# Dividing after the value products, and gathering 40 modulation dot products into the experts' loop

## The chip, the cores and the metric

The kernel runs on one core of a Trainium2 chip. The metric is the device time of one execution in microseconds (us). The engines are called as the profile calls them: PE is TensorE (PEld its weight loads), DVE is VectorE, ACT is ScalarE, POOL is GpSimd, SP is SyncE; "POOL queue" and "SP queue" are the DMA queues that POOL and SP issue to.

## The reference

Two transformer blocks of fp32 over 512 tokens of 1024 features; cut to what matters here:

```python
# first block: attention of 16 heads, 512 + 256 keys, values of 64 features
s = (einsum('bqhd,bkhd->bhqk', qn, kn) + einsum('bqhd,bkd->bhqk', qr, kr)) * ATTN_SCALE
o = einsum('bhqk,bkhd->bqhd', softmax(s), v)
y = (g_a * (o @ w_o_mla) + g_c * conformer_conv(u)) @ w_out
x = x + g1 * y
# experts: 8 heads, each with the 16 best of 128 x 128 single-neuron experts
act = gelu(einsum('thkd,td->thk', u_tab[expert], h2))
x = x + g2 * einsum('thk,thkd->td', gate * act, v_tab[expert])
x = rms_norm(x, final_g)
# second block: two layers, each a mixer and an MLP, all modulated by
mod = silu(c_2) @ ada_w + ada_b            # 2 layers x 6 x 1024
# layer 0's mixer: attention over each query's 128 best keys by an index score
# layer 1's mixer: difference of two softmaxes, by a factor from b_lambda
```

## The kernel before

Nearly all products are of fp32 operands that are split into a rounded part and the rest (`split`: ACT makes the rounded part `hi`, DVE the rest `lo`), and three matmuls make one product (`mm3`, lines 88 to 90). Weights come in chunks of 1 MB [128, 2048] through the SP queue into a ring of 2 raw tiles; three pairs of hi and lo tiles hold the split ones. The program is written as one Python pass with steps that are put in between by hand; a scheduler at build time then fixes each engine's order. The stages in order, with their place in the span: norm and latents (0 to 100 us), convolution and gate projections (to 265), first attention (267 to 500), merge (`merge` 500 to 594, `out_first` 594 to 646), choice of experts (to 790), gates and the first 80 expert tiles' activations made ahead (790 to 1190), the experts' loop (1190 to 1945), and the second block from there.

*First attention* (`attention`, line 656). Eight pairs of heads, each of 4 blocks of 128 queries times 2 heads: 64 steps. `logits` (line 709) makes a block's scores in PSUM; DVE takes the maximum (line 715), ACT the exponential with its sum (717), DVE the sum's reciprocal (718), and then ACT (line 720, for half of the steps) or DVE (line 722) scales the block. Two steps later `trans` (line 725) transposes it on PE (732), ACT copies it out (733) and, once both heads of a block are there, 12 matmuls of 128 columns bring the products with the values (742). After four blocks ACT copies the pair's result out (745). `lam_init` (line 1697), the factor of the second block's difference mixer, follows behind all heads, with the load of its row.

*Division by sums.* The second block's first attention (`dsa_attend`, line 1577) doesn't scale its probabilities: `over_sums` (line 774) divides the result of a pair. DVE makes 8 reciprocals per query, ACT spreads them over 512 columns (778), PE transposes them (782), ACT copies them out (783), and DVE multiplies (784).

*Modulation of the second block.* Layer 0's 6144 modulations are 48 dot products of the 128 partitions: one DVE instruction multiplies a [128, 1024] block of `ada_T` with the row silu(c_2), and adds up. The first 40 of them are made before layer 0 in two places: 22 in `merge` and `out_first` (`row_dots`, line 641; `dots`, line 217; the load is POOL's, 512 KB each, line 225, the product line 230; `DOT_AT` says how many at which step), and 18 in `dsa_attend` (`ws_dots`, line 145, product at line 151), whose blocks come as 9 chunks through the weights' ring. The row of silu(c_2) is made at the merge's start with a table load on ACT (line 214), and goes to scratch `sil2_d` for later use.

*The experts' loop* (`experts`, line 1196). The tokens 128 to 511 go through all 128 tiles of 128 experts: `up` multiplies the tile's activations [128, 384] with the gates (line 1239) and splits them into `ch` and `cl`; `down` makes 18 matmuls of 512 columns with the second table's chunk. The first 48 tiles of the loop also make their activations; the last 80 read theirs back (`sr`, 192 KB each on the SP queue, four tiles ahead). The first 128 tokens go another way, pick by pick (`gather_init`, line 1136): step n loads 128 rows by index on the POOL queue (line 1152) into a ring of 5 tiles, and DVE takes its dot product (1160) or adds it up (1170), four steps (`GLAG`) later. `near` (line 1253) runs `GATHER` steps beside each tile, 2.3 in the first 48 and 0.65 in the last 80; 96 steps are made ahead of the loop, and 256 are all.

## Time and profile before

| | |
|---|---|
| three timed runs | 3270.59, 3274.64, 3274.76 us, median 3274.64 |
| profiled execution | span 3265.6 us; what lies around the span isn't given |
| PE busy | 3150.1 us, 96% |
| DVE busy | 2437.2 us, 75% |
| ACT busy | 1369.8 us, 42% |
| POOL busy | 557.0 us, 17% |
| DMA | 600.71 MB, mean 184 GB/s |

A busy share is an average over stages with different limits, so it says little on one of them. A group of instructions shows its busy time, the mean duration of one, and the idle time of the engine just before them with what ended it. PE's matmuls are pipelined: the duration of one is longer than the time between two starts. A chain is followed back from the last instruction to what released it; its shares are of the stretch that it covers. "Issue" is time in which the engine waited for nothing that the profile shows.

### The profile page before, as it was taken

The numbers are of one execution on the slowest core, as the hardware profiler recorded it, in microseconds if no ns is written. First come the engines' busy times: TensorE is split into PE (matmuls) and PEld (weight loads), VectorE is DVE, ScalarE is ACT, GpSimd is POOL, SyncE is SP. The second block draws the span as 40 slices with busy tenths as digits, with TensorE's granted clock in tenths as the row PEclk, the third lists the DMA queues.
The fourth block names the chain that finished last, engine by engine and source line by source line (L and its number), as shares of the span: only waits on it lengthen the run. The fifth ranks groups of instructions, "written<-read, shape, count | busy, mean of one in ns | idle before, by whom it ended". The sixth has DMA issues, their size and how long they took to land.

```text
span 3265.6 us, 44404 instructions
## 1 busy us (share of the span) xinstructions
PE 3150.1 (96%) x17065; PEld 2701.9 (83%) x17065; DVE 2437.2 (75%) x4498; ACT 1369.8 (42%) x2093; POOL 557.0 (17%) x474
## 2 busy tenths in 40 slices
PE   6999999999999999999999999999999999899998
PEld 5787887889899999999878777769888887798887
DVE  5898899699999987777756676977566757773446
ACT  4225774333356553333333344474322245543221
POOL 1210002002232544333323310000111000000000
PEclk8999999999999999999999999999999999999999
DMA  8551016435789998888978762322566321222221
GB/s 296 187 181 46 1 40 210 176 113 188 250 306 339 321 346 305 292 294 297 328 269 300 275 220 85 110 91 91 188 214 208 132 91 63 74 96 92 78 103 65
DMA packets 181864, 600.71 MB, mean 184 GB/s; under 512 B 17009, under 2 KB 89490, under 8 KB 144659
## 3 DMA queue, kind: packets, MB, share of 16 engines
q1 hardware_dynamic: 127666, 401.76, 34.9%
q0 software_dynamic: 53984, 196.11, 16.9%
q8 instruction: 134, 2.20, 0.3%
q14 instruction: 80, 0.65, 0.1%
HBM read 550.53 MB, written 47.27 MB: 183 GB/s over the span
## 4 chain that ended last, share of the span: by engine, by line
PE 57%; DVE 17%; issue 12%; DMA 6%; ACT 3%; POOL 3%; POOLq 0%; DVEq 0%; ACTq 0%; SPq 0%
PE psp L90 10%; PE psp L88 10%; PE psp L89 10%; PE psd L89 5%; PE psd L90 5%; PE psd L88 5%; DVE lo L101 4%; DMA sr<-s_d 3%; DVE ohc L1128 3%; DVE r L1160 2%; POOL r L1152 2%; DMA r<-in_v_experts_dram,gidx 2%; PE pso L742 2%; DVE ohr L1123 2%; PE psl L88 1%
## 5 line engine op out<-in xcount | busy, mean ns | idle before, releaser
L96 ACT ACTIVATE hi<-raw 128x2048 fp32r<-128x2048 f32 (+2 forms) x263 | 500.9, 1909 | 878.3 <-PE psd L90 282.8
L101 DVE TENSOR_TENSOR lo<-raw,hi 128x2048 fp32r<-128x2048 f32 (+2 forms) x263 | 599.3, 2281 | 226.0 <-ACT hi L96 225.4
L88 PE MATMUL psp<-hT2h,hi 128*128 128x512 f32 (+1 forms) x960 | 360.6, 376 | 4.3 <-ACT r L1556 3.2
L90 PE MATMUL psp<-hT2h,lo 128*128 128x512 f32 (+1 forms) x960 | 359.8, 375 | 1.0 <-DVE lo L101 1.0
L88 PE MATMUL psu<-hT2h,hi 128*128 128x384 f32 x1024 | 356.8, 348 | 3.8 <-ACT r L962 3.8
L89 PE MATMUL psp<-hT2l,hi 128*128 128x512 f32 (+1 forms) x960 | 359.7, 375 | 0.0
L90 PE MATMUL psu<-hT2h,lo 128*128 128x384 f32 x1024 | 348.2, 340 | 0.0
L89 PE MATMUL psu<-hT2l,hi 128*128 128x384 f32 x1024 | 348.0, 340 | 0.0
L89 PE MATMUL psd<-lo,ch 128*128 128x512 f32 x768 | 306.6, 399 | 10.8 <-DVE lo L101 10.8
L90 PE MATMUL psd<-hi,cl 128*128 128x512 f32 x768 | 305.8, 398 | 0.0
L88 PE MATMUL psd<-hi,ch 128*128 128x512 f32 x768 | 305.5, 398 | 0.0
L1152 POOL DMA_INDIRECT r<-in_v_experts_dram,gidx x128 | 198.8, 1553 | 405.0 <-DVE sr L1239 189.4
L1152 POOL DMA_INDIRECT r<-in_u_experts_dram,gidx x128 | 204.0, 1594 | 353.1 <-DVE ohc L1128 130.4
L88 PEld LDWEIGHTS psp<-hT2h,hi 128*128 128x128 f32 x960 | 182.0, 190 | 39.5 <-ACT r L1556 3.6
L90 PEld LDWEIGHTS psp<-hT2h,lo 128*128 128x128 f32 x960 | 181.8, 189 | 35.9 <-DVE lo L101 1.4
L89 PEld LDWEIGHTS psp<-hT2l,hi 128*128 128x128 f32 x960 | 181.9, 189 | 34.0
L89 PE MATMUL psd<-lo,sqh 128*128 128x512 f32 x512 | 202.7, 396 | 0.0
L90 PE MATMUL psd<-hi,sql 128*128 128x512 f32 x512 | 202.7, 396 | 0.0
L88 PE MATMUL psd<-hi,sqh 128*128 128x512 f32 x512 | 202.5, 396 | 0.0
L88 PEld LDWEIGHTS psu<-hT2h,hi 128*128 128x128 f32 x1024 | 194.8, 190 | 5.8 <-ACT r L962 4.7
L89 PEld LDWEIGHTS psu<-hT2l,hi 128*128 128x128 f32 x1024 | 194.8, 190 | 1.0
L90 PEld LDWEIGHTS psu<-hT2h,lo 128*128 128x128 f32 x1024 | 194.1, 190 | 0.0
(565 smaller groups left out, 6847.0 us busy)
## 6 DMA issues: line engine op xcount, KB each, us to landing
raw<-in_u_T_dram SPq DMA_DIRECT2D x64, 1024.0 KB, 6.3
raw<-in_v_p_dram SPq DMA_DIRECT2D x64, 1024.0 KB, 5.7
raw<-in_mlp_dram SPq DMA_DIRECT2D x64, 1024.0 KB, 4.8
dotw<-in_ada_T_dram POOLq DMA_DIRECT2D x78, 512.0 KB, 4.3
gate_d<-gst SPq DMA_DIRECT2D x12, 2048.0 KB, 10.3
gt<-gate_d SPq DMA_DIRECT2D x32, 768.0 KB, 9.6
raw<-in_w_cg_dram SPq DMA_DIRECT2D x16, 1024.0 KB, 5.4
dotw<-in_w_mod_T_dram POOLq DMA_DIRECT2D x32, 512.0 KB, 4.9
```

The source lines that it names most:

```text
L88: mm(out, ah, bh, start=start, stop=False)
L89: mm(out, ah, bl, start=False, stop=False)
L90: mm(out, al, bh, start=False, stop=stop)
L96: ins = nc.scalar.activation(hi, src, AF.Copy)
L101: return nc.vector.tensor_tensor(lo, src, bf(hi), op=OP.subtract)
L742: nc.tensor.matmul(po[64 * r:64 * r + 64, qb * P:(qb + 1) * P], vg[:, kt, c:c + 64], L["PT", r][:, kt], start=kt == 0, stop=kt == 5)
L1123: V.tensor_tensor(rows, iota.unsqueeze(1).to_broadcast([P, 4, P]), pick[0][:, t0:t0 + 4].unsqueeze(2).to_broadcast([P, 4, P]), op=OP.is_equal)
L1128: V.tensor_scalar(col, iota, pick[1][:, t:t + 1], pick[2][:, t:t + 1], op0=OP.is_equal, op1=OP.mult)
L1152: ins = nc.gpsimd.indirect_dma_start(out=got[n], out_offset=None, in_=tab, in_offset=bass.IndirectOffsetOnAxis(ap=self.gidx[:, k:k + 1], a ...
L1160: ins = V.scalar_tensor_tensor(r, r, 1.0, h2, op0=OP.mult, op1=OP.mult, accum_out=act[:, k:k + 1])
```

## The change

1. The first attention leaves its probabilities as the exponential has them. Its sums stay in a tile `sum` per pair, the reciprocals and scalings of lines 718 to 722 are gone, the transposed probabilities of two blocks of queries stand side by side, so that the products with the values have 256 columns, and `over_sums` takes the place of the copy at line 745. The row of lambda is loaded at the attention's start; the scheduler now puts lambda's few instructions into the first norm, the exponential's two table loads with them.
2. `EARLY` is 0 and `MIDDLE` 40: none of the first 40 dot products is left in `merge`, `out_first` and `dsa_attend`. They are steps 256 to 295 of the gather, each a plain load of 512 KB on the POOL queue into the same ring of 5 tiles. The last 80 tiles have 1.17 steps each. The row silu(c_2) is made at the start of `experts` (a load, a sigmoid on ACT with a table load before and after it, a multiplication), and the bias of the first 16 columns is added behind the gather.
3. POOL's DMA scratch is 8192 bytes instead of the default 16384.

```diff
-FILL_P, GATHER, DOT_AT, TAPS = (16, 16, 12, 16), (2.3, 0.65), ((10,), 1, 1, 1, 2), 2
-EACT = (0, 2)
+FILL_P, GATHER, TAPS = (16, 16, 12, 16), (2.3, 1.17), 2
-EARLY = 22
-MIDDLE = range(EARLY, 40, 2)
+EARLY = 0
+MIDDLE = 40
...
     def attention(self, es_o, es_cw):
+        self.lam = self.cp.tile([P, 260], F32, name="lam")
+        self.rows_bcast(self.lam[:, :256], A["b_lambda"])
...
-                st = ep.tile([P, 3], F32, tag="st", name="st", bufs=5)
-                self.pace = nc.vector.reduce_max(st[:, 0:1], pl[:, :, :384], axis=AX.XY, negate=True)
+                st = ep.tile([P, 1], F32, tag="st", name="st", bufs=5)
+                self.pace = nc.vector.reduce_max(st, pl[:, :, :384], axis=AX.XY, negate=True)
+                if i % 8 == 0:
+                    L["sum", p] = ep.tile([P, NT, 2], F32, tag="sum", name="sum")
                 e = ep.tile([P, 2, 384], F32, tag="e", name="e", bufs=EB)
-                nc.scalar.activation(e, pl[:, :, :384], AF.Exp, bias=st[:, 0:1], accum_out=st[:, 1:2])
-                nc.vector.reciprocal(st[:, 2:3], st[:, 1:2])
-                if i % 4 in EACT:
-                    nc.scalar.activation(e, e, AF.Copy, scale=st[:, 2:3])
-                else:
-                    nc.vector.tensor_scalar(e, e, st[:, 2:3], None, op0=OP.mult)
+                nc.scalar.activation(e, pl[:, :, :384], AF.Exp, bias=st, accum_out=L["sum", p][:, qb, r:r + 1])
...
-                PT = L["PT", r] = ep.tile([P, 6, P], F32, tag="PT", name="PT", bufs=3)
+                if qb % 2 == 0:
+                    L["PT", r] = ep.tile([P, 6, 2, P], F32, tag="PT", name="PT", bufs=3)
...
-                if r == 0:
+                if i % 4 < 3:
                     return
                 po, vg = L["po"], vs[p // 2]
+                qs = slice(256 * (qb // 2), 256 * (qb // 2) + 256)
                 for kt in range(6):
                     for r in range(2):
                         c = (2 * p + r) % 4 * 64
-                        nc.tensor.matmul(po[64 * r:64 * r + 64, qb * P:(qb + 1) * P], vg[:, kt, c:c + 64],
-                                         L["PT", r][:, kt], start=kt == 0, stop=kt == 5)
+                        nc.tensor.matmul(po[64 * r:64 * r + 64, qs], vg[:, kt, c:c + 64],
+                                         L["PT", r][:, kt].rearrange("p a n -> p (a n)"), start=kt == 0, stop=kt == 5)
                 if i % 8 == 7:
-                    nc.scalar.activation(o[:, p], po, AF.Copy)
+                    self.over_sums(L.pop(("sum", p)), po, o[:, p], pst)
...
     def gather_init(self, es, h2):
+        middle = self.ada_blocks(EARLY, MIDDLE)
+        total = 2 * P + len(middle)
...
+            got[n] = self.grows.next()
+            if n >= 2 * P:
+                self.after(nc.gpsimd.dma_start(got[n], middle[n - 2 * P]), mybir.DependencyClass.Sync)
+                return
...
+            if n >= 2 * P:
+                j = EARLY + k
+                ins = V.scalar_tensor_tensor(r, r, 1.0, self.sil2, op0=OP.mult, op1=OP.mult,
+                                             accum_out=self.adac[:, 0, j:j + 1])
+                self.after(ins, mybir.DependencyClass.NoSync)
+                return
...
     def experts(self, act):
+            self.sil2 = self.row(ap, A["c_2"], tag="sil2")
             y = ap.tile([P, D], F32, name="py")
+            nc.scalar.activation(y, self.sil2, AF.Sigmoid)
+            V.tensor_tensor(self.sil2, self.sil2, y, op=OP.mult)
+            self.sil2_d = self.dram.tile([1, D], F32, name="sil2_d")
+            nc.sync.dma_start(self.sil2_d, self.sil2[0:1])
...
-                if i % 5 == 2 and i // 5 < len(MIDDLE):
-                    self.ws_dots(row, MIDDLE[i // 5])
...
-    nc = bacc.Bacc("TRN2", target_bir_lowering=False, num_devices=1)
+    nc = bacc.Bacc("TRN2", target_bir_lowering=False, num_devices=1, dynamic_dma_scratch_size=8192)
```

ACT's order within a pair of heads of the first attention, before (`psl` are scores, `e` the probabilities, `PT` the transposed ones, `pso` the products with the values, `o_T` the result):

```order
L717 ACTIVATE e,st<-psl,st 128x768
L720 ACTIVATE e<-e,st 128x768
L733 ACTIVATE PT<-pt 128x384 x2
L717 ACTIVATE e,st<-psl,st 128x768
L733 ACTIVATE PT<-pt 128x384
L717 ACTIVATE e,st<-psl,st 128x768
L720 ACTIVATE e<-e,st 128x768
L733 ACTIVATE PT<-pt 128x384
L745 ACTIVATE o_T<-pso 128x512
L733 ACTIVATE PT<-pt 128x384
```

And now, around the end of a pair (the line numbers are the changed kernel's):

```order
L698 ACTIVATE e,sum<-psl,st 128x768
L712 ACTIVATE PT<-pt 128x3x128 x2
L698 ACTIVATE e,sum<-psl,st 128x768
L712 ACTIVATE PT<-pt 128x3x128 x2
L758 ACTIVATE o_T<-sum 128x512
L712 ACTIVATE PT<-pt 128x3x128 x2
L698 ACTIVATE e,sum<-psl,st 128x768
L763 ACTIVATE o_T<-ptr 128x512
L712 ACTIVATE PT<-pt 128x3x128 x2
L698 ACTIVATE e,sum<-psl,st 128x768
```

The scaling between exponential and copy (line 720) is gone, the copy of the result (745) too, and two instructions of the division by sums stand in their place, the spreading of the reciprocals (758) and the copy of their transposes (763).

DVE's order ahead of the first head pair of `dsa_attend`, before (`raw` are chunks of the stream, `kz0l` and `kz1l` the rest parts of the first pair's keys, `dmask` and `ixm` the choice of the best keys):

```order
L151 SCALAR_TENSOR_TENSOR raw_76,adac<-raw_76,silr_17129 128x1024
...
L151 SCALAR_TENSOR_TENSOR raw_76,adac<-raw_76,silr_17129 128x1024
...
L151 SCALAR_TENSOR_TENSOR raw_75,adac<-raw_75,silr_17129 128x1024
...
L151 SCALAR_TENSOR_TENSOR raw_75,adac<-raw_75,silr_17129 128x1024
...
L1575 MATCH_REPLACE dmask<-ixm_16764,dmask 128x512
L151 SCALAR_TENSOR_TENSOR raw_76,adac<-raw_76,silr_17129 128x1024
L1564 TENSOR_SCALAR dmask<-dmask 128x512
L101 TENSOR_TENSOR kz0l<-psk,kz0h 64x512
L151 SCALAR_TENSOR_TENSOR raw_76,adac<-raw_76,silr_17129 128x1024
L101 TENSOR_TENSOR kz1l<-psk,kz1h 64x512
```

And now:

```order
L100 TENSOR_TENSOR lo_82<-raw_76,hi_79 128x2048
...
L1567 MATCH_REPLACE dmask<-ixm_16489,dmask 128x512
L1566 MAX ixm_16489<-dmask 128x8
L1567 MATCH_REPLACE dmask<-ixm_16489,dmask 128x512
L1556 TENSOR_SCALAR dmask<-dmask 128x512
L100 TENSOR_TENSOR lo_81<-raw_76,hi_78 128x2048
L100 TENSOR_TENSOR kz0l<-psk,kz0h 64x512
L1560 ISA e,st<-psl,bias 128x128
L1560 ISA st 128x1
L100 TENSOR_TENSOR kz1l<-psk,kz1h 64x512
```

The dot products (line 151) are gone from in front of the keys' rest parts; the splits of two chunks of the mixer's output weights (`lo`) have moved up to the same place.

DVE's order in the last 80 tiles of the experts' loop, before (`sr` are activations read back, `gt` gates, `cl` the activations' rest part, `lo` that of a chunk, `gacc` the sum of gathered rows):

```order
L101 TENSOR_TENSOR lo_80<-raw_76,hi_77 128x2048
L101 TENSOR_TENSOR cl_11355<-sr_11362,ch_11350 128x384
L1239 TENSOR_TENSOR sr_11361<-sr_11361,gt 128x384
L1170 SCALAR_TENSOR_TENSOR gacc<-r_8090,gact,gacc 128x1024
L101 TENSOR_TENSOR cl_11356<-sr_11363,ch_11351 128x384
L101 TENSOR_TENSOR lo_81<-raw_75,hi_78 128x2048
L1239 TENSOR_TENSOR sr_11362<-sr_11362,gt 128x384
L101 TENSOR_TENSOR cl_11357<-sr_11364,ch_11352 128x384
L1239 TENSOR_TENSOR sr_11363<-sr_11363,gt 128x384
L1170 SCALAR_TENSOR_TENSOR gacc<-r_8091,gact,gacc 128x1024
L101 TENSOR_TENSOR cl_11353<-sr_11365,ch_11348 128x384
L1239 TENSOR_TENSOR sr_11364<-sr_11364,gt 128x384
```

And now, in the part in which the dot products stand (`sil` is the row silu(c_2)):

```order
L1141 SCALAR_TENSOR_TENSOR r_7727,adac<-r_7727,sil_10979 128x1024
L1141 SCALAR_TENSOR_TENSOR r_7728,adac<-r_7728,sil_10979 128x1024
L1141 SCALAR_TENSOR_TENSOR r_7729,adac<-r_7729,sil_10979 128x1024
L100 TENSOR_TENSOR cl_10998<-sr_11005,ch_10993 128x384
L100 TENSOR_TENSOR lo_80<-raw_76,hi_77 128x2048
L1230 TENSOR_TENSOR sr_11010<-sr_11010,gt 128x384
L100 TENSOR_TENSOR cl_10999<-sr_11006,ch_10994 128x384
L1230 TENSOR_TENSOR sr_11005<-sr_11005,gt 128x384
L1141 SCALAR_TENSOR_TENSOR r_7730,adac<-r_7730,sil_10979 128x1024
L1141 SCALAR_TENSOR_TENSOR r_7731,adac<-r_7731,sil_10979 128x1024
L100 TENSOR_TENSOR cl_11000<-sr_11007,ch_10995 128x384
L1230 TENSOR_TENSOR sr_11006<-sr_11006,gt 128x384
```

Two or three dot products (line 1141) stand where one or two additions of gathered rows (line 1170) did.

## Rows read from the trace of the kernel before

**Rows 1.** Page: the span, busy time of each engine, one of its costliest groups.
```profile
span 3265.6 us, 44404 instructions
...
PE 3150.1 (96%) x17065; PEld 2701.9 (83%) x17065; DVE 2437.2 (75%) x4498; ACT 1369.8 (42%) x2093; POOL 557.0 (17%) x474
...
L101 DVE TENSOR_TENSOR lo<-raw,hi 128x2048 fp32r<-128x2048 f32 (+2 forms) x263 | 599.3, 2281 | 226.0 <-ACT hi L96 225.4
```

**Rows 2.** Busy time by stage: stretch, length; engines' busy us (count); clock, DMA share, GB/s.
```profile
281.00:499.40 218.40, 214.59 (x1687) 176.95 (x1685) 195.33 (x326) 168.87 (x335) 6.54 (x6) 1.00 0.06 23
500.00:594.00 94.00, 92.89 (x418) 76.39 (x419) 85.62 (x122) 31.64 (x30) 22.57 (x25) 1.00 0.62 215
594.00:646.00 52.00, 49.61 (x411) 48.97 (x411) 32.24 (x60) 20.65 (x41) 4.39 (x12) 1.00 0.44 152
1100.00:1200.00 100.00, 100.00 (x654) 99.13 (x653) 91.00 (x199) 57.48 (x56) 49.50 (x22) 1.00 0.92 333
1190.00:1590.00 400.00, 400.00 (x2009) 363.45 (x2008) 285.89 (x294) 137.80 (x149) 143.20 (x105) 1.00 0.85 303
1590.00:1945.00 355.00, 344.15 (x1456) 275.61 (x1455) 240.35 (x260) 114.79 (x124) 105.67 (x56) 0.99 0.83 286
```

**Rows 3.** Waits, 281 to 500 us: who waited for whom, us, times, longest.
```profile
PEld pso L742 <- issue: 9.3, 47, 0.4
PEld pso L742 <- ACT PT L733: 6.9, 25, 0.6
...
DVE lam L1703 <- DMA lam<-in_b_lambda_dram: 1.6, 1, 1.6
```

**Rows 4.** Timeline of TensorE, 433 to 435.2 us: start, duration, engine, line.
```profile
432.72 0.28 PE L89 MATMUL psv<-lo,ckvh 128*128 128x256 f32 x1
...
433.19 0.28 PE L90 MATMUL psv<-hi,ckvl 128*128 128x256 f32 x1
433.40 1.52 PE L742 MATMUL pso<-PT,vg 128*64 128x128 f32 x22
434.86 0.44 PE L88 MATMUL psl<-kcat10h,qT 128*128 128x384 f32 x1
```

**Rows 5.** Groups of 2085 to 2204 us: busy us, mean ns, idle before.
```profile
L1668 PEld LDWEIGHTS pt<-ident,e 128*128 128x128 f32 x160 | 18.9, 140 | 8.0 <-issue 2.9 <-ACT do L783 2.3 <-ACT e L1570 0.8
...
L782 PE MATMUL ptr<-ident,do 128*128 128x128 f32 x32 | 5.2, 281 | 0.7 <-ACT do L778 0.7
...
L778 ACT ACTIVATE do<-sum 128x512 f32<-128x512 f32 x8 | 5.0, 620 | 0.0
...
L784 DVE TENSOR_TENSOR do<-do,pso 128x512 f32<-128x512 f32 x7 | 4.8, 683 | 1.6 <-ACT e L1570 1.2 <-ACT do L783 0.4
```

**Rows 6.** Chain of 267 to 501 us by line, shares of 234 us.
```profile
by line: PE pso L742 22.3%; PE pt L732 14.7%; PE psl L88 10.5%; PE psl L90 9.1%; PE psl L89 8.6%; PE psq L88 3.6%; PE psq L90 2.9%; PE psq L89 2.7%; ACT e L717 2.1%; ACT PT L733 2.1%; ACT e L720 1.8%; PE psv L88 1.6%; DMA lam<-in_b_lambda_d
```

**Rows 7.** Timeline of ScalarE, about 55 us; in brackets the idle time before.
```profile
54.58 0.52 ACT L519 ACTIVATE conv_y<-psq 128x416 f32<-128x416 f32 x1 [1.24 <-PE psq L90]
```

**Rows 8.** Groups of 500 to 646 us (the merge).
```profile
L230 DVE SCALAR_TENSOR_TENSOR dotw<-dotw,silr 128x1024 f32<-128x1024 f32 x22 | 27.8, 1263 | 0.0
...
L214 ACT ACT_TABLE_LOAD x1 | 1.3, 1283 | 0.0
```

**Rows 9.** Chain of 2085 to 2205 us by line, shares of 120 us.
```profile
by line: PE pso L1677 20.8%; PE pt L1668 13.8%; PE psl L88 9.3%; PE psl L89 8.6%; PE psl L90 8.2%; ACT e L1570 6.8%; DVE raw L151 4.7%; PE ptr L782 3.0%; issue 3.0%; DVE lo L101 2.8%; PE psk L88 2.3%; PE psk L89 2.3%; PE psk L90 2.1%; DVE e
```

**Rows 10.** Waits of TensorE, 2085 to 2165 us.
```profile
PE psl L89 <- DVE kz0l L101: 4.1, 1, 4.1
```

**Rows 11.** Waits, 1590 to 1945 us (last 80 expert tiles).
```profile
DVE sr L1239 <- DMA sr<-s_d: 106.7, 42, 6.6
...
PE psd L89 <- DVE lo L101: 10.8, 6, 3.3
```

**Rows 12.** DMA, 1590 to 1945 us: GB/s in 40 slices, and the sum.
```profile
GB/s 311 400 372 340 345 242 212 302 290 239 344 261 282 234 336 266 356 246 280 290 282 283 382 235 246 249 314 269 365 258 205 270 320 225 274 293 236 305 261 213
DMA packets 54280, 101.45 MB, mean 286 GB/s; under 512 B 2992, under 2 KB 42032, under 8 KB 49328
```

More of the change, by code (lines that the diff above doesn't have):

```diff
@@ L142, in ws_split @@
             self.ws_nsplit += 1
-        self.ws_prefetch()
-    def ws_dots(self, row, j0):
-        self.ws_prefetch()
-        t = self.ws_r.pop(self.ws_i)
-        for j in range(2):
-            b = t[:, j * D:(j + 1) * D]
-            self.nc.vector.scalar_tensor_tensor(b, b, 1.0, row, op0=OP.mult, op1=OP.mult,
-                                                accum_out=self.adac[:, 0, j0 + j:j0 + j + 1])
-        self.ws_i += 1
-        self.ws_nsplit += 1
         self.ws_prefetch()
@@ L312, in build @@
             self.mods_rest()
-            dots = self.row_dots("c_2", self.ada_blocks(0, EARLY), self.adac[:, 0], es_y, "left", 2)
-            self.run(dots, DOT_AT[4])
-            self.merge(aT, dots)
+            self.merge(aT)
             xp = self.pool("x")
@@ L318, in build @@
             es_p, es_n = self.peer_open()
-            self.out_first(aT, dots)
+            self.out_first(aT)
             self.bias_rows()
@@ L344, in chunk_list @@
             L += [A[name][i] for i in range(A[name].shape[0])]
-            if name == "a_uv":
-                self.ws_plain += range(len(L), len(L) + len(MIDDLE))
-                L += [A["ada_T"][j // 2] for j in MIDDLE]
         return L
@@ L648, in first @@
             self.silu_row(name, row, dp)
-            if name == "c_2":
-                self.sil2_d = self.dram.tile([1, D], F32, name="sil2_d")
-                self.nc.sync.dma_start(self.sil2_d, row[0:1])
             steps[0]()
@@ L784, in over_sums, with merge @@
         nc.vector.tensor_tensor(dst, dst, po, op=OP.mult)
-    def merge(self, aT, dots):
+    def merge(self, aT):
         nc, A = self.nc, self.A
@@ L839, in evac_a @@
                 ln(j)
-                self.run(dots, DOT_AT[1])
             def evac_c(j, pt):
@@ L846, in evac_c @@
                 self.split(aT[0][:, j], aT[1][:, j], t, hi_eng="dve")
-                self.run(dots, DOT_AT[2])
             self.proj_T(4, aT, psp, evac_a)
@@ L870, in mods_rest, with out_first @@
                               self.pool("modr", es=es))
-    def out_first(self, aT, dots):
+    def out_first(self, aT):
         nc, A, x = self.nc, self.A, self.x
@@ L891, in evac @@
                 self.pace = nc.vector.tensor_tensor(x[t][:, cs], x[t][:, cs], y, op=OP.add)
-                if c == 2:
-                    self.run(dots, DOT_AT[3])
             def block(t):
@@ L909, in out_first @@
             self.proj_tm((1, 3), aT, psp, evac, block)
-            self.run(dots, len(dots))
             self.pace = None
@@ L1144, in gather_init @@
         V = nc.vector
+        middle = self.ada_blocks(EARLY, MIDDLE)
+        total = 2 * P + len(middle)
         got = {}
         def rows(n):
+            got[n] = self.grows.next()
+            if n >= 2 * P:
+                self.after(nc.gpsimd.dma_start(got[n], middle[n - 2 * P]), mybir.DependencyClass.Sync)
+                return
             tab, k = (A["u_experts"], n) if n < P else (A["v_experts"], n - P)
-            got[n] = self.grows.next()
             ins = nc.gpsimd.indirect_dma_start(
@@ L1173, in step @@
         def step(n):
-            if n < 2 * P:
+            if n < total:
                 rows(n)
@@ L1179, in gather_init @@
         self.pace = None
-        self.gsteps = [lambda n=n: step(n) for n in range(2 * P + GLAG)]
+        self.gsteps = [lambda n=n: step(n) for n in range(total + GLAG)]
     def after(self, ins, kind):
@@ L1272, in experts @@
             self.es_g.close()
+            V.tensor_tensor(self.adac[:, 0, :16], self.adac[:, 0, :16], self.adab[:, 0, :16], op=OP.add)
             self.bias_open()
@@ L1588, in dsa_attend @@
             v = kp.tile([P, NT, D], F32, name="dv")
-            row = kp.tile([P, D], F32, name="silr3")
-            self.rows_bcast(row, self.sil2_d)
             for r in range(2):
@@ L1699, in lam_init @@
         nc, V = self.nc, self.nc.vector
-        lam = self.lam = self.cp.tile([P, 260], F32, name="lam")
-        self.after(self.rows_bcast(lam[:, :256], self.A["b_lambda"]), mybir.DependencyClass.Sync)
+        lam = self.lam
         for i in range(2):
```

6 lines of the change are left out of this document (2 added, 4 removed).

## The prediction

> **What bounds the kernel now.** I read the page first. TensorE is busy for 96% of the span and VectorE for 75% [rows 1], so by the average only TensorE seems to matter; what the change can be worth is seen only in the six places that it touches. I read those by the table of stages [rows 2]. Its first line is the first attention: TensorE 214.59 of 218.40 us, VectorE 195.33, ScalarE 168.87. All three are near their limit, so what ends there are short waits of TensorE. The two merge lines (500 to 594 and 594 to 646) leave TensorE 1.11 and 2.39 us idle. Of the experts' loop the first 400 us leave TensorE nothing (400.00 of 400.00, DMA at 303 GB/s), while the last 355 us, in which the activations made ahead are read back, have TensorE at 344.15, VectorE at 240.35, and the DMA engines at a share of 0.83 and 286 GB/s. Then I read each place by its own view: the waits, TensorE's timeline and the chain in the attention [rows 3, 4, 6], the groups of the second block's first attention, which already divides late [rows 5], ScalarE at the start [rows 7], the dot products of the merge [rows 8], chain and waits of the second block's first attention [rows 9, 10], waits and transfers of the experts' last stretch [rows 11, 12].
>
> The profiled execution's span is 3265.6 us [rows 1]; its own time is not given apart. The median of the three runs, 3274.64, lies 9.0 above the span, and I take those 9.0 as what lies around it. A measurement of this kernel can tell about 0.2%, 6.5 us, from no change.
>
> **First attention, products with the values.** 768 products of 128 columns become 384 of 256. TensorE's timeline shows both widths side by side [rows 4]: 22 of the narrow ones start at 433.40 and the next product at 434.86, 66 ns each; the 256-column ones start every 0.1175 us (432.72 to 433.19 in four steps). 768 x 0.066 = 51.0 us become 384 x 0.1175 = 45.1: -5.9. Their weight loads besides sit idle for 9.3 us on issue and 6.9 us on the copies of the transposed probabilities [rows 3]; half the loads, half of it: -8.1, which partly is the same time. I take -7; the ends are -5.9 and -16.2 (all of it).
>
> **Its division.** 64 reciprocals and 64 scalings go, half of these on ScalarE. ScalarE's scalings (line 720) are 1.8% of the chain of 234 us [rows 6], 4.2 us. When they go the next wait there is the copies of line 733, with 2.1% in the same row, so I take half, -2.1; ends -4.2 and 0. VectorE's scalings aren't among the chain's lines shown: nothing, because reduction and exponential of the next block cover them. In return each pair of heads gets the division by sums. The second block's attention has it in the same form [rows 5]: 32 transposes, 5.2 us busy, 0.7 us of waits before them and 2.3 us of waits of the next transposes on its second copy. I take 5.2 and half of the waits, +6.7, because the first attention has the next pair's queries and keys to put in between; ends +5.2 and +8.2. For the last pair nothing covers it: the broadcast, 0.620, and the multiplication, 0.683 [rows 5], +1.3. The attention without the row of lambda: -7 - 2.1 + 6.7 + 1.3 = -1.1.
>
> **The row of lambda** is loaded at the attention's start, no longer behind its last heads, where VectorE waits 1.6 us for it [rows 3]: -1.6. Its exponential now lies in the first norm, between uses of another table, so that ScalarE loads two tables there. One load takes 1283 ns [rows 8], and ScalarE has a gap of 1.24 us at that place [rows 7]: 2.6 - 1.2 = +1.4; ends 0 and +2.6.
>
> **Merge.** 22 dot products, 27.8 us of VectorE [rows 8], and a table load leave these stages. TensorE is idle for only 3.5 us in both together [rows 2], so this is all they can give; I take -2, since some idle time ends on the normalisation itself; ends -3.5 and 0. What is saved on VectorE beyond that was covered by products.
>
> **Second block's first attention.** 18 dots and 9 transfers of 1 MB on SP's queue leave it. The dots are 4.7% of a chain of 120 us [rows 9], 5.6 us. TensorE's one long wait there, 4.1 us, is for the rest part of the first keys (kz0l) [rows 10], ahead of which VectorE's order has five dots. But in the changed order splits of chunks of the output weights have moved up to the same place, one of 2.28 us [rows 1] directly ahead of it. -5.6 + 2.3 = -3.3; ends -5.6 and 0.
>
> **Start of the experts' loop.** A row load on SP's queue, a sigmoid, one multiplication and two table loads (2.6 us, [rows 8]) are new. What queues behind them on ScalarE are the roundings of chunks and of gelu's results; with TensorE at 400.00 of 400.00 [rows 2] the chunks are split ahead of their use, and I take 0; ends 0 and +2.6. Moving the bias of 16 columns costs one small addition behind the loop: 0. The smaller scratch of POOL's DMAs: 0, because no more than five of them are in flight in the loop, by the ring of rows, which stays.
>
> **Last 80 tiles.** All 40 dots come here: 40 x 1.263 [rows 8] = 50.5 us of VectorE, and 40 x 0.524 = 21.0 MB on POOL's queue. VectorE has 115 us free, and waits 106.7 us for activations read back [rows 11], so its time has room. But the transfers rise from 101.45 MB [rows 12] to 122.4. Three ways to price that. (1) The first five slices of this very stretch mean 353.6 GB/s, one of them 400 [rows 12]; at that pace 346 us are enough, less than the 355 of today: 0. (2) TensorE's stalls on split weights, 10.8 us [rows 11], grow with the traffic (1.21) and with VectorE's load (1.21): 15.8, so +5. (3) The pace of the gates' stage, 333 GB/s at a share of 0.92 [rows 2], holds as a ceiling: 368 us, +13. I take the middle one, +5, because the pace of (3) was reached with TensorE at 100.00, which may have been what set it. Ends 0 and, if only the 303 GB/s of the loop's first part are had, +49. In the order two or three dots now stand between a tile's rest part and the next multiplication, where one or two steps of the gather were; each waits for its own row, and a late row holds up the splits behind it.
>
> The Trainium skill, page "DMA: Bandwidth & Descriptors", section "Where 436 GB/s comes from", puts the limit of HBM to SBUF transfers at about 358 GB/s per core. By that figure 122.4 MB are 342 us (an estimate), the term would be 0 and not +5, and the sum 5 us lower. The slice of 400 GB/s [rows 12] already lies above this limit, so the trace doesn't bear it out as a ceiling.
>
> **Sum:** attention -1.1, lambda -1.6 + 1.4, merge -2, second attention -3.3, experts' start 0, last tiles +5: -1.6. The span becomes 3264, the time 3273.0: no change that can be measured.
>
> **The rivals.**
> - *Slower: transfers bound the last 80 tiles.* For it: 0.83 of the DMA engines are taken now, and 1.21 times that is 1.00, where the busiest stages of the trace show 0.92 [rows 2, 12]; 42 of the waits are already for activations read back [rows 11], behind 1 MB chunks on SP's queue. Against it: slices at 340 to 400 GB/s [rows 12]. It decides once the sustained pace falls below 345 GB/s (122.4 MB in 355 us). At 333 the term is +13 and the sum -6.6 + 13 = +6.4, 3281; at 316, halfway to the first part's 303 [rows 2], 387 us, +32 and +25, 3300. Chance 0.30 that the sum passes +6.5.
> - *Faster: the loads fit into the gaps.* DMA at 353 GB/s and VectorE in its 115 us take everything, so the last tiles cost 0, and the attention gives more of the weight loads' waits (-12, halfway), -4.2 on the division and +5.2 for the new transposes: -12 - 4.2 + 5.2 + 1.3 - 1.6 + 1.4 - 3.5 - 5.6 = -19, 3256. Only the last tiles' 0 and the second attention's -5.6 give -8.9, 3266. Against it: ScalarE's copies of the transposes stay, 2.1% of the chain [rows 6]. The page's limit of the Trainium skill would give this case too. Chance 0.34.
> - *The late division does nothing.* The new transposes with all their waits, +8.2 +1.3, eat the products' -5.9 and nothing comes of the scalings: +3.6 instead of -1.1, the time 3278. For it: TensorE is busy for 98% of the stage [rows 2], and it streams as many columns of these products as before, and the transposes on top. It lies within no change; chance 0.10 of the 0.36 below.
>
> **How the numbers follow.** No change 0.36 (the forecast 0.26, the third rival 0.10), faster 0.34, slower 0.30. Predicted is the likeliest case, 3273. The range goes down to 3255, which takes in the faster case, and up to 3294, which takes in the slower one to about 322 GB/s; about 1 in 10 is left out at each end. The likeliest case alone is 3266.5 to 3279.5.
>
> **What would show it.** In the first attention: 384 products with the values, their weight loads' idle time at about 8 us, and about 1 us off the stage. Around 55 us two table loads and a gap of TensorE of about 1 us. In the second block's attention the 4.1 us before kz0l down to about 2, pairs of heads at an even pace. In the last 80 tiles a stretch of about 360 us at 340 GB/s, stalls on rest parts of about 16 us, VectorE's waits for activations read back cut by half. The prediction is wrong if that stretch passes 368 us, or keeps its length with more than 340 GB/s, or if the attention changes by more than 6 us in either direction.

## The result, and the profile after

Measured: 3289.98 us, the median of 7 runs (3280.66 to 3297.07), against 3274.64 us before (7 runs); ratio 1.0053, 95% interval 1.0039 to 1.0067. The change is slower by 0.5%: neither the forecast (3273, no change) nor the faster rival came, but the slower one, to which I had given 0.30.

The profiled execution of the changed kernel has a span of 3295.3 us, 29.7 more than that of before [rows 1], and its own time, 3297.07, lies only 1.8 above the span. So of the 9.0 us that I took as lying around the span of before, most was that execution's place among the runs: with 1.8 it took 3267.4 us (an estimate), less than any of the seven runs, while 3297.07 is the slowest of its seven. The two spans therefore differ by 29.7 and the medians by only 15.3. Stages are compared by the traces, which overstate the whole; verdicts go by the runs.

From the page of the changed kernel:

```profile
span 3295.3 us, 43622 instructions
...
PE 3156.8 (96%) x16713; PEld 2696.4 (82%) x16713; DVE 2426.6 (74%) x4418; ACT 1349.9 (41%) x2072; POOL 550.6 (17%) x492
...
L88 PE MATMUL psd<-lo,ch 128*128 128x512 f32 x768 | 310.2, 404 | 36.1 <-DVE lo L100 36.1
```

TensorE's busy time is nearly the same and the span is longer, so TensorE waits more. One group carries it: the products of the experts' second tables with the rest part of a chunk (`psd<-lo,ch`) have 36.1 us of idle time before them; before it was 10.8 [rows 11].

Where the time went is read from the first and last start of each group of products. First the kernel before, in the view of the tiles (durations min/median/max, first and last start, forms):

```profile
L742 PE MATMUL pso<-PT,vg x768: 272/273/325, 281.5 to 499.1; 128*64 128x128 f32 x192
...
L1677 PE MATMUL pso<-PT,dv x320: 272/273/325, 2101.9 to 2204.3; 128*64 128x128 f32 x160
...
L90 PE MATMUL psu<-hT2h,lo x1024: 333/337/526, 752.3 to 1585.1; 128*128 128x384 f32 x171
...
L90 PE MATMUL psd<-hi,cl x768: 392/396/629, 1214.5 to 1956.7; 128*128 128x512 f32 x192
```

Then the changed kernel:

```profile
L722 PE MATMUL pso<-PT,vg x384: 379/379/431, 289.4 to 489.3; 128*64 128x256 f32 x192
...
L1665 PE MATMUL pso<-PT,dv x320: 272/273/324, 2130.7 to 2230.9; 128*64 128x128 f32 x160
...
L89 PE MATMUL psu<-hT2h,lo x1024: 333/337/522, 745.5 to 1579.2; 128*128 128x384 f32 x171
...
L89 PE MATMUL psd<-hi,cl x768: 392/396/628, 1208.7 to 1985.9; 128*128 128x512 f32 x192
```

| from the last start of one group to that of the next | before | changed | difference |
|---|---|---|---|
| start to values of the first attention (`pso<-PT,vg`) | 499.1 | 489.3 | -9.8 |
| to the last activation product (`psu`) | 1086.0 | 1089.9 | +3.9 |
| to the loop's last product (`psd`): the last 80 tiles | 371.6 | 406.7 | +35.1 |
| to the values of the second attention (`pso<-PT,dv`) | 247.6 | 245.0 | -2.6 |
| to the end of the span | 1061.3 | 1064.4 | +3.1 |

The third line decides. (The last one holds stages in which nothing was changed; in the experiments below it lies between 1059.6 and 1064.3 us.) By stage, in the form of [rows 2], with two pieces of 15 us out of the last 80 tiles:

```profile
281.00:489.70 208.70, 203.77 (x1336) 166.00 (x1335) 179.76 (x242) 146.40 (x313) 5.91 (x4) 1.00 0.05 16
505.00:600.00 95.00, 93.95 (x482) 79.99 (x482) 62.03 (x83) 23.21 (x18) 2.84 (x3) 1.00 0.43 152
600.00:652.00 52.00, 47.58 (x377) 45.84 (x376) 25.39 (x46) 29.16 (x53) 2.70 (x9) 0.93 0.30 113
1184.00:1584.00 400.00, 400.00 (x2006) 363.35 (x2006) 286.86 (x294) 141.19 (x152) 143.17 (x105) 1.00 0.85 303
1584.00:1974.00 390.00, 353.90 (x1456) 279.47 (x1455) 288.24 (x347) 112.98 (x124) 113.85 (x96) 0.96 0.90 314
1614.00:1629.00 15.00, 15.00 (x66) 12.09 (x65) 11.81 (x14) 5.19 (x5) 8.30 (x6) 1.00 1.06 387
1809.00:1824.00 15.00, 10.04 (x33) 7.63 (x33) 11.90 (x18) 2.73 (x3) 2.36 (x4) 0.77 0.70 247
```

The attention keeps TensorE as busy as before, but takes 9.7 us less (208.70 against 218.40). The loop's first 400 us are as they were. The last stretch needs 390 us instead of 355, at 314 GB/s. At its beginning there are 15 us in which 387 GB/s are moved and TensorE never waits; later there are 15 us in which only 247 GB/s are moved, the DMA engines are at 0.70, and TensorE has 10.04 us and a granted clock of 0.77. Where TensorE stalls, the DMA engines aren't full.

Waits of that stretch, who for whom, in us, times and longest; the first two lines are those of SP's queue:

```profile
SPq L1216 <- DVE cl L100: 168.7, 42, 8.4
SPq L115 <- DVE lo L100: 119.3, 38, 8.7
...
ACT hi L95 <- DMA raw<-in_v_p_dram: 200.4, 33, 10.0
DVE sr L1230 <- DMA sr<-s_d: 88.3, 45, 6.4
...
PE psd L88 <- DVE lo L100: 36.1, 16, 5.0
```

SP can issue the load of a tile's activations (line 1216) only when VectorE has made the rest part (`cl`) that frees the ring's tile, and a chunk (line 115) only when VectorE has split the chunk two before. VectorE in turn waits 88.3 us for activations. One round of it in the timeline (start, duration, engine, instruction, in brackets the idle time before and its releaser):

```profile
1799.56 0.32 SPq L1216 DMA_DIRECT2D sr<-s_d  x1
...
1802.59 1.91 ACT L95 ACTIVATE hi<-raw 128x2048 fp32r<-128x2048 f32 x1
...
1803.25 0.55 DVE L1230 TENSOR_TENSOR sr<-sr,gt 128x384 f32<-128x384 f32 x1
1803.36 8.78 SPq L1216 DMA_DIRECT2D sr<-s_d  x2
...
1809.56 0.56 DVE L1230 TENSOR_TENSOR sr<-sr,gt 128x384 f32<-128x384 f32 x1 [4.62 <-DMA sr<-s_d]
...
1815.09 0.56 DVE L1230 TENSOR_TENSOR sr<-sr,gt 128x384 f32<-128x384 f32 x1 [2.07 <-DMA sr<-s_d]
...
1815.56 2.28 DVE L100 TENSOR_TENSOR lo<-raw,hi 128x2048 fp32r<-128x2048 f32 x1
...
1817.87 0.33 SPq L115 DMA_DIRECT2D raw<-in_v_p_dram  x1
...
1817.90 0.79 PE L88 MATMUL psd<-lo,ch 128*128 128x512 f32 x1 [4.96 <-DVE lo L100]
```

The chunk that is rounded from 1802.59 on has landed. Its rest part, 2.28 us of work, begins at 1815.56, because two multiplications with activations stand ahead of it in VectorE's order and wait 4.62 and 2.07 us for their loads, which SP issued at 1799.56 and 1803.36, the one only when a `cl` was done, the other behind a chunk that had to wait for a split. TensorE waits 4.96 us for that rest part, and SP issues the next chunk only at 1817.87.

### The profile page after: what moved, and what is told of

The parts are those of the page before. It is cut to its first block, busy times and chain, and to the rows that moved or that the text cites. A ratio compares the mean times of both kernels' runs of the same rounds, so it can differ in the third digit from the quotient of the medians.

```text
span 3295.3 us, 43622 instructions
## 1 busy us (share of the span) xinstructions
PE 3156.8 (96%) x16713; PEld 2696.4 (82%) x16713; DVE 2426.6 (74%) x4418; ACT 1349.9 (41%) x2072; POOL 550.6 (17%) x492
## 4 chain that ended last, share of the span: by engine, by line
PE 77%; DVE 9%; DMA 7%; ACT 3%; issue 2%; POOL 1%; POOLq 0%; DVEq 0%; SPq 0%; ACTq 0%
PE psp L89 10%; PE psp L87 10%; PE psp L88 10%; PE psd L88 6%; PE psd L89 6%; PE psd L87 6%; DMA sr<-s_d 5%; PE psu L87 4%; PE psu L89 4%; PE psu L88 4%; DVE lo L100 3%; PE psgt L1105 3%; PE pso L722 1%; PE psl L87 1%; PE psl L88 1%
## 5 line engine op out<-in xcount | busy, mean ns | idle before, releaser
L88 PE MATMUL psd<-lo,ch 128*128 128x512 f32 x768 | 310.2, 404 | 36.1 <-DVE lo L100 36.1
L1132 POOL DMA_INDIRECT r<-in_v_experts_dram,gidx x128 | 185.4, 1449 | 280.7 <-DVE r L1230 155.1
L88 PEld LDWEIGHTS psd<-lo,ch 128*128 128x128 f32 x768 | 146.8, 191 | 76.9 <-DVE lo L100 43.2
## 6 DMA issues: line engine op xcount, KB each, us to landing
gt<-gate_d SPq DMA_DIRECT2D x32, 768.0 KB, 10.2
```

The lines of the kernel that those rows point to most:

```text
L88: mm(out, ah, bl, start=False, stop=False)
L1132: ins = nc.gpsimd.indirect_dma_start(out=got[n], out_offset=None, in_=tab, in_offset=bass.IndirectOffsetOnAxis(ap=self.gidx[:, k:k + 1], a ...
```

## The experiments

Three theories. *A*: the rate of the transfers bounds the last 80 tiles (my slower rival). *B*: the dots' time on VectorE delays what is queued behind them. *C*: a loop bounds them, SP's issue, landing, VectorE's multiplication, rest part, and SP's next issue; more traffic makes every landing longer, and the loop adds the landings up. In E1 to E12 "the stretch" runs from the last activation product to the loop's last product, 371.6 us before and 406.7 changed. It is read from one execution of each kernel; E1, whose loop is that of before, has 369.1, so a difference of 2 or 3 us tells nothing.

**E1, late division alone.** The functions `logits` and `trans` of the change, in the kernel before, and POOL's smaller DMA scratch with them.

```diff
 (kernel before)
-                nc.vector.reciprocal(st[:, 2:3], st[:, 1:2])
...
-                    nc.scalar.activation(o[:, p], po, AF.Copy)
+                    self.over_sums(L.pop(("sum", p)), po, o[:, p], pst)
```

> The kernel before with the late division of the first attention alone (and POOL's smaller scratch); all 40 dot products and the row of lambda stay where they were. The changed kernel's trace has the attention 9.0 us shorter (its last product with the values moves from 499.3 to 489.6 us, of which 0.5 us were lost earlier). Theory A, the division brings this by itself: the same place about 8 us earlier than in the kernel before, the whole 7 to 9 us faster. Theory B, the gain came from the lambda row and from the freer VectorE of that build: less than 4 us.

Measured: 3275.74 us, ratio 0.9995 (0.9981 to 1.0009). The attention did gain:

```profile
L743 PE MATMUL pso<-PT,vg x384: 379/379/431, 290.6 to 492.2; 128*64 128x256 f32 x192
```

Its last product with the values comes at 492.2 us instead of 499.1, though its first came later by 9.1 us (290.6 against 281.5), because the products now wait for two blocks of queries. E1 also entered the attention later: the last product of the stage ahead of it (`psp<-hh,lo`) starts at 261.7 us, before at 260.0, in the changed kernel at 260.6. From there to the last product with the values it is 230.5 us, before 239.1, changed 228.7. So the late division by itself brings 8.6 of the change's 10.4 us.

But the whole isn't faster. From the last product with the values to the first one of the choice of experts (`pss`) E1 takes 173.4 us (to 665.6), the kernel before 163.3 (to 662.4), the changed one 166.3 (to 655.6). What TensorE and VectorE wait for in E1's merge:

```profile
DVE dotw L230 <- DMA dotw<-in_ada_T_dram: 7.1, 1, 7.1
...
PE psmean L831 <- DVE cdiag L829: 6.3, 1, 6.3
```

A dot product of the merge waits 7.1 us for its load; behind it on VectorE stand the normalisation's diagonal, for which TensorE waits 6.3 us, and a chunk's split. The load came late by POOL's order: POOL issues three loads from 517.75 us on, behind seven of its additions that take 15.85 us in one piece, while in the kernel before an issue (513.24) stands between the third and the fourth of them. So theory A of this run is right on the place and wrong on the whole. It does not follow that the dots as such cost the merge 10 us: the kernel before has them too and takes 163.3. E1 shows that its own order of POOL loses what the attention won; no run has the late division, the dots and POOL's old order together.

**E2 and E3, the two halves of an added dot.** E2 leaves out the 40 loads (so the modulations' values), E3 all but 8 of each product's 1024 columns.

```diff
 (E2)
-                self.after(nc.gpsimd.dma_start(got[n], middle[n - 2 * P]), mybir.DependencyClass.Sync)
 (E3)
-                ins = V.scalar_tensor_tensor(r, r, 1.0, self.sil2, op0=OP.mult, op1=OP.mult,
+                ins = V.scalar_tensor_tensor(r[:, :8], r[:, :8], 1.0, self.sil2[:, :8], op0=OP.mult, op1=OP.mult,
```

> The changed kernel without the 40 loads of 512 KB: the 40 dot products run on what the ring's tiles hold (the loads and so the modulations' values are left out). Stretch looked at: from the last activation product to the loop's last product, 371.7 us in the kernel before, 406.7 in the changed one. Theory A, transfers bound it: back to 372 +-5. Theory B, the dots' time on VectorE delays what is queued behind them: stays at 400 or more. Theory C, a loop of both (SP issues the next activations and chunks only after VectorE is done with older ones, so landing time and VectorE's work add up): in between, 380 to 392.

> The changed kernel with its 40 loads, but each dot product only over the first 8 of 1024 columns (the rest of the product is left out), so that VectorE has 47 us less and the transfers are the same. The same stretch, 406.7 us: theory A, transfers bound it: stays at 402 or more. Theory B, VectorE's time: back to 372 +-5. Theory C, the loop of landing time and VectorE's work: 380 to 395.

E2 took 3263.74 us (ratio 0.9949, 0.9929 to 0.9969), E3 3298.13 (1.0046, 1.0028 to 1.0063). The last starts, of E2 and then of E3:

```profile
L89 PE MATMUL psu<-hT2h,lo x1024: 331/337/525, 745.7 to 1579.6; 128*128 128x384 f32 x171
...
L89 PE MATMUL psd<-hi,cl x768: 389/396/632, 1209.0 to 1956.3; 128*128 128x512 f32 x192
```

```profile
L89 PE MATMUL psu<-hT2h,lo x1024: 332/337/522, 743.6 to 1585.9; 128*128 128x384 f32 x171
...
L89 PE MATMUL psd<-hi,cl x768: 392/396/628, 1215.3 to 1988.4; 128*128 128x512 f32 x192
```

The stretch is 376.7 us without the loads and 402.5 without the dots. Theory B falls: 47 us of VectorE's time are worth about 4 us, the loads 30. By the numbers that I had written down this is theory A's case, not C's.

**E4, activations read back earlier.**

```diff
-            srd = Ring(self.pool("srd", es=es), 6, [P, TD], F32, "sr")
+            srd = Ring(self.pool("srd", es=es), 8, [P, TD], F32, "sr")
...
-                load_act(n + 4)
+                load_act(n + 6)
```

> The changed kernel with the activations read back six tiles ahead instead of four (a ring of eight), nothing else. Theory A, the rate of the transfers bounds it: the stretch stays at 400 or more. Theory C, the loop SP's issue, landing, VectorE bounds it: two more tiles of slack take most of VectorE's waits for activations (88 us) away, and the stretch falls to 380 to 392. If it falls not at all, the loop over the two raw chunk tiles (issue after the split of the chunk before last) is what is left of theory C.

3290.06 us, ratio 1.0037 (1.0022 to 1.0052): by the runs as slow as the change. The stretch is 396.1 us (1582.2 to 1978.3), below theory A's 400 and above theory C's 392, so by the numbers written down it decides nothing. The order that came of it says more: the multiplications had moved ahead by two tiles too, close behind the issue of their loads again (median from issue to multiplication, k-th against k-th in the timelines, 8.8 us, in the changed kernel 7.8), and VectorE still waited 79.1 us for activations.

**E5 and E6, the same work elsewhere in the loop**, by the numbers of steps beside a tile: (2.3, 1.17) becomes (3.15, 0.67) and (2.7, 0.93).

> The changed kernel with 3.15 steps beside each of the first 48 tiles and 0.67 beside each of the last 80 (instead of 2.3 and 1.17): the 40 steps more lie where TensorE was never short of data (303 GB/s, TensorE 400.00 of 400.00). Two stretches: first products of the loop to the last activation product, 371.4 us in both kernels; from there to the loop's last product, 371.7 before and 406.7 changed. Theory A, the load of the transfers on the last stretch cost the 35 us and the first stretch has room (it would carry about 356 GB/s, and the first 60 us of the changed kernel's last stretch carried 385 to 392 with TensorE busy all the time): first stretch 371 to 375, last one 372 +-5, the whole 3250 to 3262. Theory B, any place with 350 GB/s stalls: first stretch 385 to 400, the whole 3270 to 3290.

> The changed kernel with 2.7 and 0.93 steps: half of the 40 steps more beside the first 48 tiles, half beside the last 80. Theory A: the first stretch stays at 371 to 373, the last one has half of the additional transfers and lands between, 380 to 392. Theory B: both stretches lengthen by 8 us or more.

E5 took 3275.20 us, ratio 1.0009 (0.9993 to 1.0026), E6 3289.41, ratio 1.0049 (1.0031 to 1.0068). Last starts of E5, then of E6:

```profile
L89 PE MATMUL psu<-hT2h,lo x1024: 333/337/522, 747.0 to 1589.7; 128*128 128x384 f32 x171
...
L89 PE MATMUL psd<-hi,cl x768: 389/396/792, 1209.8 to 1968.4; 128*128 128x512 f32 x192
```

```profile
L89 PE MATMUL psu<-hT2h,lo x1024: 333/337/525, 742.0 to 1576.2; 128*128 128x384 f32 x171
...
L89 PE MATMUL psd<-hi,cl x768: 392/396/796, 1205.6 to 1977.5; 128*128 128x512 f32 x192
```

E5's stretch is 378.7 us, and its first 48 tiles lose 9 (TensorE has 380.04 of 387 us there): as much as the attention had won. Both lie outside theory A's ranges, the first stretch (379.9) outside theory B's too; of the numbers written down only B's for the whole came. E6 is the telling one: half of the additional loads cost 401.3 - 371.6 = 29.7 us, all of them 35.1, and by the runs E6 is as slow as the change. That isn't proportional to the bytes, as theory A would have it (380 to 392), and the first 48 tiles, 370.6 us, didn't lengthen, as theory B would.

**E8, E5 with E4's deeper ring**: steps of (3.15, 0.67), a ring of eight and activations read back six tiles ahead. It was meant to be the fastest version; theory A expected a stretch of 360 to 368 us and 3245 to 3256 for the whole. It took 3278.36 us, ratio 1.0009 (0.9992 to 1.0026), with a stretch of 377.4 us, no better than E5. VectorE still waits 97.9 us for activations there (103.9 in E5). Reading back earlier brings nothing here either.

**E7, fewer loads in flight**: `GLAG` 2 instead of 4, the ring of rows 3 instead of 5.

> The changed kernel with the product two steps behind its load instead of four, in a ring of three tiles instead of five, so that POOL has at most three loads of 512 KB in flight. Theory A1, the additional loads delay what TensorE waits for by being many at a time (up to 2.5 MB of rows that are wanted later, beside a chunk of 1 MB and activations that are wanted at once): last stretch 385 to 398. Theory A2, it is the sum of the bytes alone: 403 to 410. If rows now come too late, VectorE waits for them and everything gets longer, the gates' stage too.

3384.12 us, ratio 1.0348 (1.0307 to 1.0388): everything in the loop is longer, the last stretch by 25 us more and the first 48 tiles by 41. The rows now come too late themselves (in the last stretch VectorE waits 46.6 us for gathered rows, in the changed kernel 3.0), so the run says nothing about A1 and A2; that question stays open.

**E9 to E12, the loop opened.** Nothing is taken away or added; a tile's multiplication is put behind the rest part of the tile three before it (E9; two in E11, four in E12), where the scheduler had it behind that of the tile five before. With a ring of six that was one tile's time behind the issue of its load. E10 is the same in the kernel before.

```diff
-                self.split(*s, r)
+                cls[n] = self.split(*s, r)
+                if n - 3 in cls and i < AHEAD:
+                    self.behind(self.mult, cls[n - 3])
```

> The changed kernel, with nothing but VectorE's order changed in the last 80 tiles: a tile's multiplication with the gates stands behind the rest part (cl) of the tile three before it, where it stood behind that of the tile five before it. The ring of six tiles gives a load only when the rest part six tiles before is done, so the multiplication came about one tile (4.2 us) behind the issue of its load, which takes 6.6 us to land; VectorE waited 88 us so, and the splits of chunks queued behind those waits (rounding's end to start of the rest part 7.2 us), while SP can issue a chunk only when the split of the one two before is done. Theory C, this loop is the bound and the added transfers stretch it: VectorE's waits for activations under 25 us, rounding to rest part under 3 us, the last stretch 345 to 360 instead of 406.7, the whole 3228 to 3245. Theory A, the rate of the transfers is the bound: the stretch stays at 395 or more.

> The same order in the kernel before. Theory C: its loop is relieved too, the last stretch from 371.7 to 342 to 355, the whole 20 to 30 us faster than before. The difference to E9 then tells what the change is worth without this loop: theory C expects E9 to be faster by 8 to 14 us (the attention's 9, the second attention's 4). Theory A: no change (TensorE's stalls there were 10.8 us, at most that is won).

> E9 with the multiplication behind the rest part of the tile two before. The load has a tile more to land (12.6 to 16.8 us), but the rounding of the multiplied tile has less time ahead of its products. Theory C: within 5 us of E9, either way.

> E9 with the multiplication behind the rest part of the tile four before: the load has two tiles (8.4 us) to land, little over the 6.6 us of the median. Theory C: between E9 and the changed kernel, stretch 355 to 390.

| | median, us | ratio to before (95%) | stretch, us |
|---|---|---|---|
| E9 | 3245.29 | 0.9902 (0.9870 to 0.9933) | 354.9 |
| E10 | 3255.81 | 0.9942 (0.9922 to 0.9963) | 355.0 |
| E11 | 3242.68 | 0.9902 (0.9872 to 0.9932) | 355.0 |
| E12 | 3247.63 | 0.9933 (0.9903 to 0.9963) | 357.8 |

E9's last starts, its stretch, the wait, the chain by line and the DMA's pace:

```profile
L89 PE MATMUL psu<-hT2h,lo x1024: 332/337/525, 745.3 to 1579.0; 128*128 128x384 f32 x171
...
L89 PE MATMUL psd<-hi,cl x768: 392/396/399, 1208.4 to 1933.9; 128*128 128x512 f32 x192
```

```profile
1573.00:1932.00 359.00, 358.71 (x1555) 290.09 (x1554) 300.02 (x368) 126.73 (x149) 123.93 (x99) 1.00 0.97 353
```

```profile
DVE sr L1230 <- DMA sr<-s_d: 37.2, 14, 6.0
```

```profile
by line: PE psd L87 31.7%; PE psd L88 31.7%; PE psd L89 31.7%; ACT nh L253 1.5%; issue 0.6%; PE psu L89 0.6%; PE psu L88 0.6%; PE psu L87 0.6%; PE psn L236 0.3%; ACT hT2h L95 0.3%; DVE x L268 0.2%; POOL rms L276 0.2%; ACT z L274 0.1%; DVE r
```

```profile
GB/s 317 226 374 402 376 403 383 376 391 371 354 362 384 373 408 375 362 383 356 359 384 395 392 388 342 410 338 408 370 357 396 385 399 374 403 288 287 321 137 2
```

TensorE has 358.71 of 359 us, the chain is its products and nothing else, and the DMA engines carry 353 GB/s, all the additional loads among them. Theory C's numbers hold for the stretch (345 to 360 expected); VectorE's wait is 37.2 us where under 25 was expected, and it no longer matters. The time from the end of a chunk's rounding to the start of its rest part, worked out from the timelines (the k-th rounding against the k-th rest part, mean over the stretch), was some 6.5 us before, 7 changed, and is 1.8 in E9. Landings have not become shorter: chunks take 10.2 us (median) and activations 10.4, in the changed kernel 7.7 and 6.6. But the multiplication now comes 13.4 us behind the issue of its load (median; 7.8 in the changed kernel), and so VectorE's queue seldom stands on a load. The stretch of E10:

```profile
1584.00:1944.00 360.00, 359.42 (x1557) 289.99 (x1556) 254.67 (x284) 130.52 (x152) 99.61 (x59) 1.00 0.86 293
```

E10 has TensorE as full at 293 GB/s. With and without the 40 loads and dots the stretch is the same 355 us. The loop through VectorE's order is shown as the bound, and the rate of the transfers, up to these 353 GB/s, isn't one. What isn't shown is the second half of theory C, that longer landings are what the added loads lengthen the loop by: E6's chunks landed in 6.9 us and its activations in 6.4, as in the kernel before (6.7 and 6.4), and its stretch was 401.3 us all the same.

All four beat both kernels, E9 and E11 that of before by 1%. E9's whole is just above the 3228 to 3245 expected; E10 gained 16.7 us where 20 to 30 were expected. E9 is 10.5 us faster than E10, within the 8 to 14 expected: that is what the change is worth once the loop is open. E11 and E12 lie where they were expected.

## Why the prediction was wrong

- *The step that failed: the price of the last 80 tiles*, +5 us where +35.1 came in the traces. By the medians it is about 28 (an estimate: opening the loop gains 44.7 us in the changed kernel, 3289.98 to 3245.29, and 16.7 before, 3272.47 to 3255.81, and leaves both with the same stretch). I scaled TensorE's stalls of 10.8 us by the traffic and VectorE's load, and I counted VectorE's 106.7 us of waits for activations as room. What the runs showed in its place is a loop in which these waits are the bound, since the splits that TensorE and SP need stand behind them in VectorE's order. It was closed already in the kernel before: SP waited there 127.8 us to issue the next chunk until a split was done, and the chain of the last 80 tiles went through the loads of activations for 30.7% of 355 us. In the changed kernel it is 44.7% of 390:

```profile
SPq L116 <- DVE lo L101: 127.8, 39, 9.0
...
by line: DMA sr<-s_d 30.7%; PE psd L89 14.6%; PE psd L90 14.3%; PE psd L88 14.1%; issue 10.2%; DVE lo L101 5.3%; DVE cl L101 3.1%; DMA r<-in_v_experts_dram,gidx 2.9%; DVE gacc L1170 2.1%; DMA raw<-in_v_p_dram 2.0%; POOL r L1152 0.9%; DVE sr
```

```profile
by line: DMA sr<-s_d 44.7%; DVE lo L100 9.0%; issue 7.9%; PE psd L88 6.4%; PE psd L89 6.4%; PE psd L87 6.3%; DVE cl L100 4.1%; DVE r L1141 3.9%; DVE gacc L1156 3.7%; DMA r<-in_ada_T_dram 2.7%; DMA raw<-in_v_p_dram 2.4%; DVE sr L1230 1.0%; A
```

How the loads lengthen the closed loop stays open: E6's landings were as short as before, and it lost nearly as much.
- *The range* up to 3294 holds the measured 3289.98, but it went that far for the slower rival alone, whose reason was wrong: that is luck. Of the signs that I had named, the stretch beyond 368 us (390) and the attention's change by more than 6 came; VectorE's waits for activations weren't cut by half (88.3), and the stalls on rest parts were 36.1 us, not about 16.
- *The slower rival* named the right stretch and sign, and its 316 GB/s are near the 314 measured, but its reason was wrong. Its limit of 345 GB/s doesn't exist here: E9 carries 353 on the mean. The low rate was the effect of the stalls, not their cause. (Halfway between 333 and 303 is 318, not 316; it moves the rival's time by about 2 us.) What I had called the case against it, slices of 340 to 400 GB/s [rows 12], was right. The limit of about 358 GB/s that I cited from the Trainium skill's page "DMA: Bandwidth & Descriptors" isn't borne out by E9 either: most of its slices of 9 us lie above it, up to 410, and from 1591 to 1905 us it carries 374 on the mean.
- *First attention*: right in mechanism, too small. I had -1.1 and -1.6 for lambda; the attention is 10.4 us shorter. The products with the values I took at -7: their own busy time in the stage fell from 65.56 to 54.45 us, by 11.1, within my bound of -16.2. The division's transposes I took at +6.7, half of their waits included: they are busy for 4.72 us, and the next transposes' weight loads wait only 0.3 us on the division's second copy, so that +5 would have been nearer. (VectorE with 195 and ScalarE with 169 of the stage's 218 us weren't near their limit, as I had written.)
- *Start*: two table loads, +1.4 forecast. By 260 us the changed kernel is 0.6 us late, but E1 is 1.7 and E10 1.4 late at the same place, and neither moved lambda; so the term is smaller than what executions differ by.
- *Merge*: -2 forecast, +3.0 came: 163.3 us before and 166.3 changed from the last product with the values to the first of the choice of experts. E10, which keeps the dots there, has 163.2 and E9, which doesn't, 166.1. So nothing was won there against the kernel before. At the end, where it does wait, it waits 2.7 us for the normalisation and 1.7 for the bias rows, before 1.2 and 2.2. No run separates what lengthened this end; it stays open.
- *Second attention*: -3.3 forecast, -2.6 measured from the loop's end; the wait for kz0l fell from 4.1 to 2.1 us. The split that moved up in the order was the right reason for not taking all of 5.6.
- *Experts' start*: 0 forecast; the loop's first 400 us are unchanged, TensorE 400.00.
- *"Late division does nothing"* was wrong, E1's place shows it, though its whole looks as if it were right.

## What to carry to other kernels

A load that is prefetched four tiles ahead in the program may still be used one tile after its issue, if its ring's tile comes free late and the scheduler places the first use early; compare issue, landing and use in the trace, not the program's distance. Where an engine executes in order, a wait that costs that engine nothing can still be the bound, by what is queued behind it and by the issue that this releases. Before work is moved onto a stretch with a loop of this kind, open the loop: here three lines gave 17 us before, and 45 with the change.

## What was not expected of the hardware

A stall of TensorE costs more than itself. The granted clock was 1.00 in the 15 us from 1614 on, without a stall, and 0.77 in those around the stall of 4.96 us: a product behind it takes 0.63 us in the timeline (the lines below) where one ahead of it took 0.40, and until 1823.18 us products start 0.43 us apart instead of 0.23, that is, TensorE fell to the lower of its two levels, 1.2 GHz, for some 5 us.

```profile
1812.55 0.40 PE L87 MATMUL psd<-hi,ch 128*128 128x512 f32 x1
...
1818.49 0.63 PE L89 MATMUL psd<-hi,cl 128*128 128x512 f32 x1
```

Over the whole stretch it can be counted, since the products are the same (before, changed, E9):

```profile
1585.10:1956.70 371.60, 360.47 (x1529) 288.69 (x1528) 250.45 (x275) 127.34 (x149) 106.78 (x58) 0.99 0.80 278
1579.20:1985.90 406.70, 370.46 (x1530) 292.79 (x1529) 297.93 (x361) 125.63 (x149) 114.95 (x98) 0.97 0.87 306
1579.00:1933.90 354.90, 354.61 (x1529) 285.60 (x1528) 294.87 (x363) 126.68 (x149) 122.62 (x98) 1.00 0.96 351
```

Of the 35.1 us between the first two, 25.1 are idle time of TensorE, and 10.0 are the products themselves, at a granted clock of 0.97 instead of 0.99.

And the DMA engines, which I had thought near their end at 0.92 and 333 GB/s, stood at 0.97 with 353 GB/s for 359 us beside a TensorE that never waited.
